# A short matmul of 144 columns ahead of each row of groups of seven products, one of 112 columns in each half of the quads, and the quads' split weights 64 bytes further into their tiles

## The chip, the core and the metric

The kernel runs on one core of one Trainium2 chip. The metric is the time of one execution on the device in microseconds (us). Of the five engines, TensorE (PE, the matrix unit, whose weight loads are listed apart as PEld), VectorE (DVE) and ScalarE (ACT) do the arithmetic; GpSimd (POOL) and SyncE (SP) start transfers (DMAs).

## What is computed

Two layers of a decoder trunk on 512 tokens of width 1024, all in float32. The parts that this document speaks of are the two feed-forward blocks (FFN) of each layer and the mixer's branch gates:

```python
def swiglu(h, w_gate, w_up, w_down):
    return (jax.nn.silu(h @ w_gate) * (h @ w_up)) @ w_down
...
    for l in range(DEPTH):
        h = rms_norm(x, gn[0])
        x = x + 0.5 * rms_norm(swiglu(h, w_ffn1_gate[l], w_ffn1_up[l], w_ffn1_down[l]), gn[1])
        h = rms_norm(x, gn[2])
        proj = h @ w_in[l]
...
        mixed = jax.nn.sigmoid(gate_a) * y_hg + jax.nn.sigmoid(gate_b) * y_at
        x = x + rms_norm(mixed @ w_out[l], gn[3])
        h = rms_norm(x, gn[4])
        x = x + 0.5 * rms_norm(swiglu(h, w_ffn2_gate[l], w_ffn2_up[l], w_ffn2_down[l]), gn[5])
```

D_FF is 2816, that is 22 blocks of 128 columns. Between the two FFNs of a layer stands the mixer: a gated recurrence and a windowed attention, each followed by a projection and a gate.

## The kernel before

**One product is three matmuls.** A float32 matrix is held as a high part (`whi` for weights, rounded to the type fp32r) and a low part (`wlo`, what is left). `mm3` multiplies high by high, high by low and low by high. Each matmul loads its own 128x128 weight block first, so 13531 matmuls come with 13531 weight loads.

**Weights.** `Stream` reads them from memory in tiles `w` of 128x1024 floats by DMAs on SP's queue (four raw buffers, `W32`), and `Stream.split` makes of each an `Item`: a pair `whi`, `wlo` of eight blocks of 128 columns, with six buffers each (`WS`). ACT writes `whi` (line 353). `wlo` comes from a subtraction on DVE (line 362, kinds u, b, c) or from a negated copy on ACT (line 357) and an accumulating DMA that POOL starts (line 360, kinds v, a, d). The tile of an item has 1088 columns, and `at` says at which column the 1024 begin: `pairs` puts its items (kinds a, b, c, d) 16 columns, that is 64 bytes, in (`ASIDE`); `plain` puts its items at column 0.

**Stages.** An FFN begins with a *quad*: four output blocks of 128 columns for all tokens, from four plain items. Where the input was normalised by the stage before (three of the four FFNs, and both mixers), `quad` runs in two halves of 256 tokens, 96 matmuls of 256 columns each, the weights being used twice; late in the first half TensorE turns the second half of the tokens (`turn`). The first FFN does its quad on all 512 tokens. After the quad come a few single blocks (`project`, 512 columns), and then a *row of groups*: `fast` calls `sevenths` once for each further block of D_FF, 15 times in the first FFN and 19 times in the three others. One group makes the gate and the up block with seven products of half size in place of eight: it is 7 x 4 x 3 = 84 matmuls of 256 columns, from four items. The operands that are sums of input quarters come from `pre.sums()` ahead of the row, the sums of weights from DVE inside `split`, and the sums of results from DVE at the end of `sevenths` (lines 1054 to 1061). The order on TensorE is written out by hand; in a row the order on DVE and ACT is held to the program's order too (`hold`, `tight`). After the row comes the down projection (`down`), 512 columns wide, part of which again uses seven products, with sums on DVE (lines 263, 295, 432).

The mixer has a quad, projections, attention and recurrence, and four groups (`branches`), each followed by two products of 512 columns; these groups are single ones, each a row of its own.

In time, the rows of groups of the four FFNs run from 88.6 to 237.0, 729.3 to 915.3, 1063.8 to 1249.0 and 1745.4 to 1933.4 us of the profile. They are called row 1 to row 4 here.

Of the kernel before, what the change touches and what calls it, by code (L numbers as in the profile page):

```python
# [15 lines left out]
P = 128  # L16
# [16 lines left out]
    first=0.0, spread=2300.0, squares=1700.0, lay=34500.0, laid=770.0, normed=7600.0, final=2600.0,  # L33
# [4 lines left out]
TURN = 0  # L38
SEVEN = 16
ASIDE = 16  # L40
ORDER = ("p1", "p3", "p7", "p2", "p6", "p5")
HEADS = (0, 4, 1, 5, 2, 6, 3, 7)

# [2 lines left out]
def trunk(ctx: ExitStack, tc: tile.TileContext, xin, wall, gains, lbT, hgain, sinks, c_dist, c_mask, c_ident, out):  # L46
# [12 lines left out]
    def nm(s):  # L59
        seq[0] += 1  # L60
        return f"{s}_{seq[0]}"

    def big(dt=F32, shape=None):
        return sb.tile(shape or [P, S], dt, tag="s", name=nm("s"), bufs=SLOTS)
# [4 lines left out]
    def acc():  # L69
        return ps.tile([P, S], F32, tag="acc", name=nm("acc"), bufs=5)  # L70

    def aux():
        return ps.tile([P, S], F32, tag="aux", name=nm("aux"), bufs=3)
# [40 lines left out]
    def mm(o, lhsT, rhs, start, stop):  # L114
        nc.tensor.matmul(o, lhsT, rhs, start=start, stop=stop)  # L115
        n = 1
        for d in rhs.shape[1:]:
            n *= d
        if rhs.dtype == F32:
            order.t += max(n / 2.4, 27.0) * (2 if lhsT.shape[1] == 64 and n < 256 else 4)  # L120
        else:
            order.t += max(n / 2.4, 107.0)
# [35 lines left out]
    class Stream:  # L158
# [10 lines left out]
            self.side, self.freed = [], 0  # L169
            self.part = {}  # L170

        def plain(self, n, kind="u"):
            self.items += [Item(kind, self.n + i) for i in range(n)]
            for i in range(n):
                self.src.setdefault(self.n + i, self.wall + i)
            self.n += n
            self.wall += n

        def pairs(self, n, at=ASIDE):

            for _ in range(n):
                self.items += [Item(k, self.n, 4 if k == "d" else 8, at) for k in "abcd"]
                for i in range(2):
                    self.src.setdefault(self.n + i, self.wall + i)
                self.n += 2
                self.wall += 2

        def gates(self):
# [6 lines left out]
            self.plain(1)  # L195

        def rows(self, kt, fast):


# [15 lines left out]
            if fast:  # L215
# [6 lines left out]
                def product(k):  # L222
                    for q in range(n):
                        it = Item(k, u, 4)
                        it.q, it.n = q, n
                        self.items.append(it)

                for k in ORDER:
                    product(k)
# [179 lines left out]
    ws = Stream()  # L409

    def mm3(o, st, mv, start, stop):

        mm(o, st[0], mv[0], start, False)
        mm(o, st[0], mv[1], False, False)
        mm(o, st[1], mv[0], False, stop)

    def wmm(o, b, mv, start, stop, poll=True):

        mm3(o, b[2:], mv, start, stop)
        ws.used(b)  # L420
        if poll:
            order.poll()

    def cut(pair, c):
        return pair[0][:, c], pair[1][:, c]
# [222 lines left out]
    class Late:  # L648
# [42 lines left out]
        def leave(self, n, k):  # L691
# [4 lines left out]
            elif n in (5, 7):  # L696
                (self.x37 if n == 7 else self.x56)[k] = None

    def down(src, kt, l, n, nxt, fast):


# [292 lines left out]
    def quad(pre, halves):  # L994

        o = [acc() for _ in range(4)]
        blocks = {}
        ws.pinned = halves
        for half in (0, 1) if halves else (None,):
            c = WHOLE if half is None else HALF[half]  # L1000
            for k in range(KT):
                order.until(lambda: pre.have[half or 0] > k)
                for j in range(4):
                    if (k, j) not in blocks:
                        blocks[k, j] = ws.next(uses=2 if halves else 1)
                    wmm(o[j][:, c], blocks[k, j], cut(pre.h[k], c), k == 0, k == KT - 1)
            ws.pinned = False
        return o
# [17 lines left out]

    H2 = S // 2

    def sevenths(pre, between=lambda: None):

        def product(o, it, c, n):
            x = pre.operand(n)
            for k in range(4):
                wmm(o, ws.block(it, c + k), x[k], k == 0, k == 3)

        p1, p26, p57, p43 = acc()[:, :H2], acc(), acc(), aux()
        s, v = big()[:, :H2], big(F32, [P, 2, H2])
        w = ws.whole()  # L1040
        product(p1, w, 0, 1)
        ws.hold(nc.scalar.copy(s, p1))
        product(p26[:, :H2], w, 4, 2)
        between()
        w = ws.whole()
        product(p57[:, :H2], w, 0, 5)
        product(p57[:, H2:], w, 4, 7)
        c = ws.whole()
        product(p26[:, H2:], c, 0, 6)
        ws.product()  # L1050
        m = sb.tile([P, 4, H2], F32, tag="m", name=nm("m"), bufs=1)
        pairs = [p.rearrange("p (i t) -> p i t", i=2) for p in (p26, p57, p43)]

        ws.hold(nc.vector.tensor_tensor(m[:, 0:4:2, :], pairs[0], s.unsqueeze(1).to_broadcast([P, 2, H2]), op=ALU.add))

        ws.hold(nc.vector.tensor_tensor(v, pairs[1], m[:, 2:3, :].to_broadcast([P, 2, H2]), op=ALU.add))
        product(p43[:, :H2], c, 4, 4)
        product(p43[:, H2:], ws.whole(), 4, 3)

        ws.hold(nc.vector.tensor_tensor(m[:, 3, :], p57[:, :H2], v[:, 1, :], op=ALU.add))  # L1060
        ws.hold(nc.vector.tensor_tensor(m[:, 1:3, :], pairs[2], v[:, ::-1, :], op=ALU.add))
        return m

    def fast(pre, a, start):
        def early():
            if j == FT - 1:
                for i in range(SEVEN, SEVEN + EARLY):
                    ws.part[i] = split(a[i])

        ws.tight = True  # L1070
        for j in range(start, FT):
            ws.most = AHEAD + (j < FT - 1)
            m = sevenths(pre, early)
            z = big(F32, [P, 2, H2])
            ws.hold(nc.scalar.activation(out=m[:, 0:2, :], in_=m[:, 0:2, :], func=AF.Silu))

            def gate(m=m, z=z):
                ws.hold(nc.vector.scalar_tensor_tensor(z, m[:, 0:2, :], -1.0, m[:, 2:4, :], op0=ALU.mult, op1=ALU.mult))

            ws.gate = gate  # L1080
            if j == FT - 1:
                ws.product()
            a.append(z.rearrange("p i t -> p (i t)"))
        ws.tight = False

    def ffn(l, n, pre, nxt, halves=True):
# [13 lines left out]

        first = isinstance(pre, First)
        o = quad(pre, halves)
        if first:
            o.append(project(pre))
# [152 lines left out]
    def mixer(l, pre, nxt):  # L1257
# [40 lines left out]
        def run(i, heads):  # L1298
# [8 lines left out]
            for n in range(2):  # L1307
                order.spawn(outputs(i + n, box[n]), n * WAIT["apart"])

        o = quad(pre, True)  # L1310
        order.spawn(run(0, [head(o[2 * i], o[2 * i + 1], i) for i in range(2)]))

# [125 lines left out]
        def branches(get):  # L1438

            v = sevenths(pre)  # L1440
            src = get()
            for i in range(2):
                g = big(F32, [P, 2, H2])
                nc.scalar.activation(out=g, in_=v[:, 2 * i : 2 * i + 2, :], func=AF.Tanh, scale=-0.5 if i else 0.5)
                p = acc()
                for k in range(4):
                    wmm(p, ws.next(), src[k], k == 0, k == 3)
                g = g.rearrange("p i t -> p (i t)")
                nc.vector.scalar_tensor_tensor(g, g, 1.0, p, op0=ALU.add, op1=ALU.mult)
                yield g  # L1450
# [23 lines left out]
    for l in range(DEPTH):  # L1474
        for n in (0, 2, 4):
            if n == 2:
                ws.plain(4, "v")
                ws.plain(2 * H + 2 + 8 + LATE * 3 // 2)
                for _ in range(KT - LATE // 2):
                    ws.gates()  # L1480
                ws.rows(KT, False)
            else:
                p = FIRST if l + n == 0 else 3
                ws.plain(4, "v" if l and not n else "u")
                ws.plain(min(2 * p, 8) - 4)
                ws.plain(max(2 * p - 8, 0), "v")
                ws.pairs(FT - p)
                ws.rows(FT, True)
    pre = First()
# [68 lines left out]
    for l in range(DEPTH):  # L1558
        pre = ffn(l, 0, pre, (l, 2), halves=l > 0)
        pre = mixer(l, pre, (l, 4))  # L1560
        pre = ffn(l, 4, pre, (l + 1, 0) if l + 1 < DEPTH else None)
# [81 lines left out]
```

## Time and profile before

| | us |
|---|---|
| median of 3 runs | 2056.75 |
| lowest and highest | 2055.87, 2056.76 |
| the profiled execution | 2057.03 |
| its span in the profile | 2055.3 |
| TensorE busy | 2044.0 |
| weight loads busy | 1831.3 |
| DVE busy | 1624.1 |
| ACT busy | 1250.1 |
| clock granted to TensorE | full in all 40 slices |

The span runs from the first to the last recorded instruction; 1.7 us of the execution lie around it. A matmul's bar in the profile is longer than the distance to the next one, since matmuls overlap in the engine's pipeline, so a busy TensorE says nothing of its pace. The pace is read from the starts: the timeline gives the start of each matmul, and the view by stretches counts the matmuls of a stretch (it counts those that reach into it too, about two more than begin in it).

### The profile page before, as it was taken

To read this page: it belongs to the slowest core of one execution; us is meant where nothing else is said; L and a number is where in the kernel's file an instruction comes from. 1 tells how busy PE (TensorE), PEld (TensorE's weight loads), DVE (VectorE), ACT (ScalarE), POOL (GpSimd) and SP (SyncE) were. 2 spreads that over 40 slices of the span, in tenths; PEclk is the share of its full clock that TensorE was granted. 3 is DMA by queue.
4 is the path that set the end of the run, shared out by engine and by line. 5 is a ranking of instruction groups with operands and counts; after the bars stand their busy time and mean duration, and the time that the engine had idled before them with its cause. 6 is when DMAs were issued, how large, how long until landed. Compare 5 with 4: busy or idle time off the path is not lost. (4 is left out here: it accounts for less than half of the span.)

```text
span 2055.3 us, 36503 instructions
## 1 busy us (share of the span) xinstructions
PE 2044.0 (99%) x13531; PEld 1831.3 (89%) x13531; DVE 1624.1 (79%) x2894; ACT 1250.1 (61%) x2213; POOL 267.6 (13%) x318
## 2 busy tenths in 40 slices
PE   9999999999999999999999999999999999999998
PEld 7899988877888999997899998888778989999987
DVE  5887889767676778888988788977686858788888
ACT  7556687446355556658866566864554545665684
POOL 0111140000000012113201111400000100111140
PEclk9999999999999999999999999999999999999999
DMA  8587798312247367879857778872122563788794
GB/s 256 148 188 191 175 206 239 114 64 70 73 101 207 113 151 189 189 187 208 206 151 189 192 187 207 177 232 85 62 73 62 140 193 99 181 189 195 176 199 123
DMA packets 166802, 328.07 MB, mean 160 GB/s; under 512 B 19072, under 2 KB 85088, under 8 KB 166624
## 3 DMA queue, kind: packets, MB, share of 16 engines
q1 hardware_dynamic: 122416, 228.16, 33.3%
q0 software_dynamic: 44064, 97.54, 28.2%
q8 instruction: 106, 1.74, 0.4%
q14 instruction: 72, 0.59, 0.1%
q10 hardware_dynamic: 144, 0.05, 0.0%
HBM read 213.43 MB, written 14.73 MB: 111 GB/s over the span
## 5 line engine op out<-in xcount | busy, mean ns | idle before, releaser
L115 PE MATMUL acc<-s,whi 128*128 128x256 f32 (+1 forms) x4976 | 1035.9, 306 | 0.4 <-ACT whi L353 0.4
L115 PEld LDWEIGHTS acc<-s,whi 128*128 128x128 f32 x4976 | 799.7, 189 | 47.2 <-issue 3.2
L115 PE MATMUL acc<-s,wlo 128*128 128x256 f32 (+1 forms) x2488 | 760.5, 306 | 1.0 <-DMA wlo<-w 0.8
L115 PEld LDWEIGHTS acc<-s,wlo 128*128 128x128 f32 x2488 | 468.9, 188 | 25.1 <-DMA wlo<-w 1.5
L115 PE MATMUL acc<-whi,s 128*128 128x512 f32 x1360 | 442.0, 393 | 1.4 <-DVE s L432 1.3
L353 ACT CAST whi<-w 128x1024 fp32r<-128x1024 f32 (+1 forms) x310 | 286.4, 928 | 151.0 <-PE acc L115 102.9
L353 ACT CAST whi<-tt 128x1024 fp32r<-128x1024 f32 x160 | 167.9, 1049 | 250.7 <-DVE tt L347 177.8
L360 POOL DMA_DIRECT2D wlo<-w x178 | 154.0, 867 | 1237.3 <-ACT wlo L357 532.0
L115 PEld LDWEIGHTS acc<-whi,s 128*128 128x128 f32 x1360 | 255.2, 188 | 59.6 <-issue 3.2
L362 DVE TENSOR_TENSOR wlo<-tt,whi 128x1024 fp32r<-128x1024 f32 x160 | 196.0, 1225 | 131.6 <-ACT whi L353 124.6
L115 PE MATMUL acc<-wlo,s 128*128 128x512 f32 x680 | 266.3, 392 | 1.2 <-DVE wlo L295 1.2
L115 PE MATMUL aux<-s,whi 128*128 128x256 f32 (+1 forms) x1296 | 233.1, 281 | 0.0
L362 DVE TENSOR_TENSOR wlo<-w,whi 128x1024 fp32r<-128x1024 f32 (+1 forms) x132 | 157.6, 1207 | 75.6 <-ACT whi L353 74.6
L115 PEld LDWEIGHTS aux<-s,whi 128*128 128x128 f32 x1296 | 199.1, 189 | 1.1 <-issue 0.5
L115 PE MATMUL aux<-s,wlo 128*128 128x256 f32 (+1 forms) x648 | 182.2, 281 | 0.0
L115 PEld LDWEIGHTS acc<-wlo,s 128*128 128x128 f32 x680 | 127.7, 188 | 30.0 <-DVE wlo L295 5.2
L357 ACT ACTIVATE wlo<-w 128x1024 fp32r<-128x1024 f32 (+1 forms) x178 | 153.7, 863 | 0.0
L115 PE MATMUL aux<-whi,s 128*128 128x512 f32 x432 | 143.8, 390 | 0.0
L443 POOL DMA_DIRECT2D s<-s x128 | 111.0, 969 | 218.4 <-ACT s L431 98.6
L115 PEld LDWEIGHTS aux<-s,wlo 128*128 128x128 f32 x648 | 121.9, 188 | 0.3
L295 DVE TENSOR_TENSOR wlo<-s,whi 128x512 fp32r<-128x512 f32 x160 | 103.0, 690 | 9.9 <-ACT whi L287 8.1
L431 ACT CAST s<-s 128x512 fp32r<-128x512 f32 (+1 forms) x140 | 70.8, 548 | 44.8 <-DVE s L490 39.3
(184 smaller groups left out, 2468.8 us busy)
## 6 DMA issues: line engine op xcount, KB each, us to landing
w<-wall SPq DMA_DIRECT2D x267, 512.0 KB, 4.2
wlo<-w POOLq DMA_DIRECT2D x98, 512.0 KB, 5.2
w<-wall SPq DMA_DIRECT2D x224, 128.0 KB, 3.6
wlo<-w POOLq DMA_DIRECT2D x80, 256.0 KB, 3.2
s<-wall SPq DMA_DIRECT2D x128, 128.0 KB, 4.1
s<-s POOLq DMA_DIRECT2D x64, 256.0 KB, 4.6
x_d<-s SPq DMA_DIRECT2D x48, 256.0 KB, 4.2
s<-x_d SPq DMA_DIRECT2D x48, 256.0 KB, 5.2
```

The lines of the kernel that those rows point to most:

```text
L115: nc.tensor.matmul(o, lhsT, rhs, start=start, stop=stop)
L295: pin(nc.vector.tensor_tensor(it.lo[:, h[c]], w[c], it.hi[:, h[c]].bitcast(F32), op=ALU.subtract))
L353: i = nc.scalar.copy(it.hi[:, c], w[:, c])
L357: i = nc.scalar.mul(it.lo[:, c], w[:, c], -1.0)
L360: nc.gpsimd.dma_start(it.lo[:, c].bitcast(F32), w[:, c], accum_op=ALU.add)
L362: self.hold(nc.vector.tensor_tensor(it.lo[:, c], w[:, c], it.hi[:, c].bitcast(F32), op=ALU.subtract))
L431: (hold or ws.hold)(nc.scalar.copy(hi, src))
L443: nc.gpsimd.dma_start(lo.bitcast(F32), src, accum_op=ALU.add)
```

## The change

```diff
+LEAD, LEAD_IN = 144, 112
...
-        def plain(self, n, kind="u"):
-            self.items += [Item(kind, self.n + i) for i in range(n)]
+        def plain(self, n, kind="u", at=0):
+            self.items += [Item(kind, self.n + i, at=at) for i in range(n)]
...
                 for j in range(4):
                     if (k, j) not in blocks:
                         blocks[k, j] = ws.next(uses=2 if halves else 1)
+                    if halves and (k, j) == (0, 2):
+                        lead(o[j][:, c], blocks[k, j][2], pre.h[k][0][:, c], LEAD_IN)
                     wmm(o[j][:, c], blocks[k, j], cut(pre.h[k], c), k == 0, k == KT - 1)
...
-    def sevenths(pre, between=lambda: None):
+    def lead(o, st, mv, n):
+        mm(o[:, :n], st, mv[:, :n], True, True)
+
+    def sevenths(pre, between=lambda: None, first=True):
...
         w = ws.whole()
+        if first:
+            lead(p1, w.hi[:, :P], pre.operand(1)[0][0], LEAD)
         product(p1, w, 0, 1)
...
-            m = sevenths(pre, early)
+            m = sevenths(pre, early, j == start)
...
-                ws.plain(4, "v")
+                ws.plain(4, "v", ASIDE)
...
-                ws.plain(4, "v" if l and not n else "u")
+                ws.plain(4, "v" if l and not n else "u", ASIDE if l + n else 0)
```

`lead` is one more matmul, with the same weight block and the first columns of the same input as the matmul behind it, and into the same accumulator, which that matmul then starts afresh; so its result is overwritten. It stands ahead of the first group of each FFN's row (4 times) and ahead of each group of the mixers (8 times) with 144 columns, and ahead of the third block's first product in each half of the five quads that run in halves (10 times) with 112 columns. The four items of these five quads now begin at column 16 of their tiles. The quad of the first FFN stays as it was.

On DVE, ACT, POOL and SP the instructions stand in the same order as before, and on TensorE nothing is moved but for the 22 added matmuls. This is TensorE at the start of row 1, where the 512 columns of the last `project` end and the first group begins (`s` is the input, 880 and 918 are two accumulators), before:

```order
L115 MATMUL acc_880<-s_186,wlo_704 128x512
L115 MATMUL acc_880<-s_199,whi_703 128x512
L115 MATMUL acc_880<-s_200,whi_703 128x512
L115 MATMUL acc_880<-s_199,wlo_704 128x512
L115 MATMUL acc_918<-s_598,whi_766 128x256 x2
L115 MATMUL acc_918<-s_598,wlo_767 128x256
L115 MATMUL acc_918<-s_623,whi_766 128x256 x2
```

and now:

```order
L116 MATMUL acc_880<-s_186,wlo_704 128x512
L116 MATMUL acc_880<-s_199,whi_703 128x512
L116 MATMUL acc_880<-s_200,whi_703 128x512
L116 MATMUL acc_880<-s_199,wlo_704 128x512
L116 MATMUL acc_918<-s_598,whi_766 128x144
L116 MATMUL acc_918<-s_598,whi_766 128x256 x2
L116 MATMUL acc_918<-s_598,wlo_767 128x256
L116 MATMUL acc_918<-s_623,whi_766 128x256 x2
```

One matmul of 144 columns stands between the last wide one and the first of the group. And this is TensorE in the second quad of the program, at the start of its first half (4133 to 4136 are the four accumulators, 4029 and 4030 the input's high and low part), before:

```order
L115 MATMUL acc_4133<-s_4029,whi_3918 128x256
L115 MATMUL acc_4133<-s_4030,whi_3918 128x256
L115 MATMUL acc_4133<-s_4029,wlo_3919 128x256
L115 MATMUL acc_4134<-s_4029,whi_3918 128x256
L115 MATMUL acc_4134<-s_4030,whi_3918 128x256
L115 MATMUL acc_4134<-s_4029,wlo_3919 128x256
L115 MATMUL acc_4135<-s_4029,whi_3918 128x256
L115 MATMUL acc_4135<-s_4030,whi_3918 128x256
```

and now (all numbers of names are one higher):

```order
L116 MATMUL acc_4134<-s_4030,whi_3919 128x256
L116 MATMUL acc_4134<-s_4031,whi_3919 128x256
L116 MATMUL acc_4134<-s_4030,wlo_3920 128x256
L116 MATMUL acc_4135<-s_4030,whi_3919 128x256
L116 MATMUL acc_4135<-s_4031,whi_3919 128x256
L116 MATMUL acc_4135<-s_4030,wlo_3920 128x256
L116 MATMUL acc_4136<-s_4030,whi_3919 128x112
L116 MATMUL acc_4136<-s_4030,whi_3919 128x256
L116 MATMUL acc_4136<-s_4031,whi_3919 128x256
```

Six matmuls run first, then the one of 112 columns, then the quad goes on as it did.

## The prediction

> **What bounds the kernel now.** I read the page first, then the timeline of TensorE for its pace, then the counts by stretch, then DVE and ACT beside it.
>
> ```profile
> span 2055.3 us, 36503 instructions
> PE 2044.0 (99%) x13531; PEld 1831.3 (89%) x13531; DVE 1624.1 (79%) x2894; ACT 1250.1 (61%) x2213; POOL 267.6 (13%) x318
> ```
>
> TensorE hardly ever stands still, so what counts is how far apart its matmuls start. The same matmul of 256 columns has three paces. Below, from the timeline (start, length, engine, line, operation, tiles, shape, count), are the first and last line of a stretch in row 1, one in row 2 and one in a quad:
>
> ```profile
> 205.15 0.40 PE L115 MATMUL aux<-s,whi 128*128 128x256 f32 x2
> ...
> 211.51 0.40 PE L115 MATMUL acc<-s,whi 128*128 128x256 f32 x2
> ...
> 790.29 0.39 PE L115 MATMUL acc<-s,whi 128*128 128x256 f32 x2
> ...
> 796.41 0.39 PE L115 MATMUL aux<-s,whi 128*128 128x256 f32 x2
> ...
> 348.48 0.40 PE L115 MATMUL acc<-s,whi 128*128 128x256 f32 x2
> ...
> 355.68 0.40 PE L115 MATMUL acc<-s,whi 128*128 128x256 f32 x2
> ```
>
> Row 1: 54 matmuls in 6.36 us, 117.8 ns each. Row 2: 54 in 6.12 us, 113.3 ns. Quad: 60 in 7.20 us, 120.0 ns. Nothing waits inside these stretches and the clock is full; only the quad's weights begin at column 0 of their tiles. So 117.8 and 113.3 are two paces of the same work, and the counts by stretch show when they change:
>
> ```profile
> 88.60:237.00 148.40, 148.40 (x1262) 1.00 0.79 191
> 602.50:612.20 9.70, 9.70 (x86) 1.00 0.96 240
> 760.00:788.00 28.00, 28.00 (x248) 1.00 0.81 193
> 790.00:845.00 55.00, 55.00 (x488) 1.00 0.81 191
> 847.00:915.00 68.00, 68.00 (x580) 1.00 0.79 193
> 1125.00:1199.00 74.00, 74.00 (x655) 1.00 0.81 192
> 1221.00:1249.00 28.00, 28.00 (x240) 1.00 0.75 188
> 1745.40:1933.40 188.00, 188.00 (x1597) 1.00 0.78 189
> ```
>
> With two taken off each count, rows 1 and 4 run at 117.8 from end to end; row 2 runs at 113.8 and 113.2 between 760 and 845 and at 117.6 afterwards; row 3 at 113.3 from 1125 and at 117.6 from 1221. Each change stands at a place where a weight load was late; one of them (weight loads, the idle time before in brackets):
>
> ```profile
> 788.70 0.19 PEld L115 LDWEIGHTS acc<-s,wlo 128*128 128x128 f32 x1 [0.81 <-DMA wlo<-w]
> 788.80 0.30 PEld L115 LDWEIGHTS acc<-s,whi 128*128 128x128 f32 x2
> ```
>
> So the pace is set by a phase that an interruption deals anew and undisturbed work keeps. A lead of another length is such an interruption, without a wait. That is what the change can act on.
>
> **But a faster TensorE runs into DVE.** In a row DVE and ACT prepare the weights in turns, and each group shows the same loop:
>
> ```profile
> 741.44 0.68 DVE L1054 TENSOR_TENSOR m<-acc,s 128x512 f32<-128x512 f32 x1
> ...
> 746.29 1.23 DVE L362 TENSOR_TENSOR wlo<-tt,whi 128x1024 fp32r<-128x1024 f32 x1 [0.59 <-ACT whi L353]
> ...
> 750.04 1.22 DVE L362 TENSOR_TENSOR wlo<-tt,whi 128x1024 fp32r<-128x1024 f32 x1 [1.19 <-ACT whi L353]
> 751.18 0.68 DVE L1054 TENSOR_TENSOR m<-acc,s 128x512 f32<-128x512 f32 x1
> ...
> 799.71 0.68 DVE L1054 TENSOR_TENSOR m<-acc,s 128x512 f32<-128x512 f32 x1
> ...
> 809.42 0.68 DVE L1054 TENSOR_TENSOR m<-acc,s 128x512 f32<-128x512 f32 x1
> ```
>
> Line 1054 comes once a group: 9.74 us apart where TensorE ran at 117.8, 9.71 where it ran at 113.3. A group of 84 takes TensorE 9.89 us at the one pace and 9.52 at the other. The loop, which waits for ACT and not for TensorE, lies between. It also keeps its place from row to row:
>
> ```profile
> 729.33 0.40 PE L115 MATMUL acc<-s,whi 128*128 128x256 f32 x2
> ...
> 909.26 0.68 DVE L1061 TENSOR_TENSOR m<-aux,s 128x512 f32<-128x512 f32 x1
> ...
> 1745.44 0.40 PE L115 MATMUL acc<-s,whi 128*128 128x256 f32 x2
> ...
> 1925.35 0.68 DVE L1061 TENSOR_TENSOR m<-aux,s 128x512 f32<-128x512 f32 x1
> ```
>
> The same late sum of DVE stands 179.93 us behind the start of row 2 and 179.91 behind that of row 4, though row 2 spent half its time at 113.3 and ended 186.0 us after its start, row 4 188.0. What row 2 had won it gave back in the down projection. The first 53 us of the four down projections, by count (TensorE, weight loads, DVE, ACT, POOL):
>
> ```profile
> 237.00:290.00 53.00, 53.00 (x235) 43.88 (x235) 46.58 (x94) 38.88 (x82) 16.42 (x19) 1.00 0.86 204
> 915.30:968.30 53.00, 52.07 (x228) 42.16 (x227) 46.84 (x94) 37.31 (x80) 15.30 (x18) 1.00 0.85 206
> 1249.00:1302.00 53.00, 51.56 (x223) 41.16 (x222) 47.96 (x94) 37.15 (x78) 14.11 (x17) 1.00 0.86 206
> 1933.40:1986.40 53.00, 53.00 (x236) 43.90 (x235) 45.80 (x92) 37.43 (x80) 15.76 (x19) 1.00 0.85 205
> ```
>
> Behind rows 1 and 4 TensorE gets 235 and 236 matmuls done, behind the two that ran partly at 113.3 228 and 223. At 227 ns each (53 us over 234) that is 1.6 and 2.8 us of waiting, for DVE:
>
> ```profile
> 942.43 0.30 PEld L115 LDWEIGHTS acc<-whi,s 128*128 128x128 f32 x2 [1.04 <-DVE s L432]
> ...
> 946.96 0.19 PEld L115 LDWEIGHTS aux<-wlo,s 128*128 128x128 f32 x1 [0.62 <-DVE wlo L295]
> ```
>
> So in an FFN the bound is already DVE's and ACT's chain, with TensorE close on its heels.
>
> **The change, part by part.** *The leads* add 22 matmuls. A lead waits for the accumulator, weights and input for which the matmul behind it waits anyway, so no wait is added, and no DMA and nothing on POOL's or SP's queue moves. Each loads weights, so it costs at least the 0.10 us between two crowded weight loads (788.70 to 788.80 above) and at most a product at the worst pace, 0.12. I take 0.11: 0.9 us in the mixers' rows, 1.1 in the quads, 0.4 in the FFN rows.
>
> *The quads.* 10 halves x 96 = 960 matmuls, now at 120.0. With the weights 64 bytes in they are in the rows' situation, so 113.3 or 117.8: a gain of 6.4 or 2.1 us for all, 1.28 or 0.43 a quad. I take 113.3, since a lead stands in each half. Less 0.22 for two leads that is 1.06 a quad. In the two mixers I let all of it count, 2.1 us: TensorE has hardly a gap there. In the three FFNs DVE must follow, and only part of its chain hangs on the quad. It waits for the turned tokens in the middle of the quad, then is held by ACT:
>
> ```profile
> 703.79 0.88 DVE L629 SCALAR_TENSOR_TENSOR s<-acc,g_sb,s 128x256 fp32r<-128x256 f32 x2 [0.63 <-PE aux L125]
> ...
> 712.40 1.29 DVE L432 TENSOR_TENSOR s<-s,s 128x512 fp32r<-128x512 f32 x2 [1.39 <-ACT s L431]
> ```
>
> The first wait has 0.63 us to give; the turn comes after 72 of the faster matmuls, 0.5 us earlier. I take 0.6 a quad, 1.8 for three. Quads together 3.9 us, bounded by 0 (DVE does not move, the mixers wait too) and 5.3 (all of it counts).
>
> *The mixers' groups.* Eight of 84, of which one ran at 113.3 already (602.50 to 612.20 above, 84 in 9.7 us with a wait in it). Seven x 84 x 4.44 ns = 2.6 us, less 0.9 for leads: 1.7. Bounds: -0.9 (the lead changes nothing) and 1.7 (nothing waits).
>
> *The FFN rows.* TensorE alone would win 5.6 us in row 1 (15 groups x 0.37), 7.1 in row 4, 5.1 in row 2 and 4.3 in row 3, whose stretches at 113.3 count already. DVE's loop stops this at 9.71 us a group, and the down projection takes most of the rest, as in rows 2 and 3. Row 2 is the measure: it came out of its row 2.0 us earlier than row 4 and lost 1.6 behind it. I give 0.4 to row 4, the same and 1.0 more to row 1, where the loop starts with more lead and TensorE never waits, 0.6 to row 3 for the bigger wait, nothing to row 2: 2.4 us. The leads are hidden here behind the same DVE work; were DVE's cover gone they would cost 0.4. Bounds: 0 and 22.
>
> Sum: 3.9 + 1.7 + 2.4 = 8.0 us off the profiled execution's 2057.03: 2049.0. That execution lies 0.3 us above the median of 2056.75, less than the sum is good for.
>
> **The rivals.** *A. TensorE is the bound after all.* For it: 99% busy. Then the rows keep their 22, the mixers 1.7, the quads 5.3, less 0.4: 2028. Against it: what became of row 2's gain. Chance 0.07.
>
> *B. The leads do not set the pace.* A late load does not always bring 113.3 (at 847 and 1221 it brought 117.6), and nothing in the trace says what 144 or 112 columns do. Then only the offset acts: 2.1 us less 2.4 for leads, no change, 2057; or one of the two leads works and the other not: 2053. Chance 0.17, most of it within 2052 to 2057.
>
> *C. Weights and inputs do not disturb each other at all, the paces have another cause, and the 64 bytes do nothing.* Then 22 x 0.11 = 2.4 us is all that remains: 2059.4. Against it: 120.0 in the quads beside 117.8 in the rows, with the same shapes. Chance 0.06. [...]
>
> *D. Slower: a lead locks a row into the quads' 120.0.* Then a group takes 10.08 us, more than DVE's loop of 9.71, and TensorE is the bound again. From 9.89 that is 0.19 x 15 = 2.8 us in row 1, 3.6 in row 4, 4.0 in row 2, which had kept 0.4, 3.6 in row 3, which had kept nothing, 1.9 in the mixers' groups and 2.4 for leads, the quads staying as they are: 18.3, so 2075. It decides from the first group on. Against it: no group at offset 16 shows 120 anywhere. Chance 0.06.
>
> **The numbers.** My forecast has 0.64: 2049.0, in its own range from 2042 (the quads' 5.3, row gains of 8) to 2054 (half the quads' gain, nothing from the rows). The range for 8 in 10 leaves out A, C and D, 0.19: 2041 to 2056.5. 0.2%, or 4.1 us, is about what a measurement of this kernel can tell from no change. Faster by more: 0.60 of my 0.64, A's 0.07, 0.07 of B: 0.74. Slower by more: D's 0.06 and 0.03 from C, were a lead to cost three times as much: 0.09. Within: 0.17.
>
> **What would show it.** The rows, counted by stretch, should run at 113.3 ns from their first group, with late loads of `wlo<-w` in rows 1 and 4 too, which have none now. Line 1054 on DVE should still come every 9.71 us. The first 53 us of all four down projections should hold 223 to 229 matmuls, with waits for lines 432 and 295. The quads should show 113.3 behind their leads. I am wrong if line 1054 comes closer together than 9.7 us or the down projections show no wait (then A), if rows start at 117.8 (B), or if quads stay at 120.0 (C).

## The result, and the profile after

| | before | after |
|---|---|---|
| median of 20 runs each, us | 2056.44 | 2052.96 |
| lowest and highest | 2055.45, 2057.69 | 2051.33, 2053.96 |
| ratio, 95% interval | | 0.9983 [0.9976, 0.9989] |
| the profiled execution | 2057.03 | 2052.22 |
| its span | 2055.3 | 2050.4 |

The change makes the kernel 3.5 us faster. That is 0.17%: the interval of the ratio excludes no change, but the median lies inside the band of 0.2% that the prediction called "within" and gave 0.17, against 0.74 for a gain beyond it. The forecast was 2049.0, 8.0 us below the profiled execution of before; by the medians less than half of that came. In the two profiled executions the difference is 4.8 us, because the one of before happened to lie 0.6 us above its median and the one of after 0.7 below; the parts below are counted in these two.

The first lines of the page of after (busy time, share of the span, instructions):

```profile
span 2050.4 us, 36557 instructions
PE 2035.9 (99%) x13553; PEld 1820.7 (89%) x13553; DVE 1623.6 (79%) x2894; ACT 1250.1 (61%) x2213; POOL 267.6 (13%) x318
```

TensorE has 22 matmuls more and is busy for 8.1 us less, while DVE's busy time is the same. Where it went is read by stage. These are the four rows of after and the first 53 us behind each (stretch, its length, TensorE, weight loads, DVE, ACT, POOL, then granted clock, DMA share, GB/s):

```profile
88.60:233.40 144.80, 144.80 (x1262) 144.80 (x1261) 116.08 (x163) 89.09 (x122) 24.95 (x29) 1.00 0.79 191
233.40:286.40 53.00, 51.70 (x225) 41.49 (x224) 47.55 (x94) 37.30 (x79) 14.72 (x17) 1.00 0.85 205
728.10:915.20 187.10, 186.94 (x1599) 186.42 (x1598) 150.43 (x210) 115.12 (x158) 31.85 (x37) 1.00 0.78 188
915.20:968.20 53.00, 52.69 (x232) 42.89 (x231) 46.85 (x95) 38.36 (x81) 16.13 (x19) 1.00 0.88 213
1062.30:1247.00 184.70, 182.66 (x1599) 181.52 (x1598) 147.71 (x208) 113.16 (x156) 31.84 (x37) 1.00 0.77 187
1247.00:1300.00 53.00, 50.90 (x221) 40.59 (x220) 48.40 (x95) 37.43 (x78) 13.86 (x16) 1.00 0.86 211
1741.60:1927.90 186.30, 185.73 (x1598) 185.23 (x1597) 149.62 (x210) 115.03 (x158) 31.84 (x37) 1.00 0.78 189
1927.90:1980.90 53.00, 52.25 (x229) 42.30 (x229) 46.74 (x94) 37.35 (x79) 15.35 (x18) 1.00 0.85 208
```

Row 1 takes 144.8 us where it took 148.4. But behind it TensorE gets 225 matmuls done in 53 us, where it got 235 before. Row 4 takes 186.3 (188.0 before), and 229 matmuls follow (236 before). Rows 2 and 3 are about as long as they were (1.1 us longer and 0.5 shorter).

Stage by stage, from the starts of the first matmuls of the stages in both timelines (a row counts with its down projection, up to the next stage):

| us against before | forecast | measured |
|---|---|---|
| row 1 and behind it | -1.4 | -0.35 (row -3.6, behind it +3.2) |
| row 2 and behind it | 0 | +0.06 (row +1.1, behind it -1.0) |
| row 3 and behind it | -0.6 | -0.38 |
| row 4 and behind it | -0.4 | -0.92 (row -1.6, behind it +0.7) |
| five quads | -3.9 | -2.19 (-0.44 each) |
| first mixer, second mixer | -1.7 in all | -0.09 and -1.00 |
| sum | -8.0 | -4.8 (with +0.04 ahead of row 1) |

**The paces of a row.** The counts of after, by pieces of the four rows (two matmuls are to be taken off each count, as before):

```profile
88.60:183.00 94.40, 94.40 (x834) 94.40 (x833) 75.83 (x107) 57.67 (x78) 17.21 (x20) 1.00 0.79 189
190.00:233.40 43.40, 43.40 (x370) 43.40 (x370) 34.52 (x49) 26.78 (x38) 6.02 (x7) 1.00 0.80 194
...
788.00:915.00 127.00, 127.00 (x1081) 127.00 (x1080) 103.31 (x144) 78.54 (x108) 21.53 (x25) 1.00 0.78 190
...
1123.00:1245.00 122.00, 121.89 (x1072) 121.50 (x1071) 97.98 (x139) 73.93 (x101) 21.53 (x25) 1.00 0.80 193
...
1743.00:1760.00 17.00, 17.00 (x152) 17.00 (x151) 12.66 (x19) 9.93 (x15) 2.98 (x4) 1.00 0.73 155
1762.00:1799.00 37.00, 37.00 (x317) 37.00 (x316) 30.37 (x43) 23.20 (x32) 6.88 (x8) 1.00 0.79 185
1801.00:1857.00 56.00, 56.00 (x494) 56.00 (x495) 45.84 (x65) 34.94 (x48) 10.32 (x12) 1.00 0.78 188
1859.00:1927.00 68.00, 68.00 (x578) 68.00 (x579) 54.82 (x77) 42.76 (x60) 11.18 (x13) 1.00 0.77 190
```

Row 1 starts at 113.5 ns a matmul (832 in 94.4 us) and ends at 117.9. Row 4 starts at 113.3, goes at 117.5 from 1762, at 113.8 from 1801 and at 118.1 from 1859. Both were at 117.8 from end to end before. Row 2 starts at 113.3 too, but from 788 to its end it goes at 117.7 (1079 in 127 us), where before it had kept 113.3 until 846; that is why it is longer now. Row 3 starts at 113.3 and never leaves it: its 122 us from 1123 on hold 1070 matmuls and a few short waits. Four of the ten weight loads that the profile lists as late in the rows and the groups of the mixers (idle time before them in brackets), one in the first mixer's second group, one in row 3 and two in row 4:

```profile
602.42 0.19 PEld L116 LDWEIGHTS acc<-s,wlo 128*128 128x128 f32 x1 [0.67 <-DMA wlo<-w]
...
1110.94 0.19 PEld L116 LDWEIGHTS acc<-s,wlo 128*128 128x128 f32 x1 [0.51 <-DMA wlo<-w]
...
1761.15 0.19 PEld L116 LDWEIGHTS acc<-s,wlo 128*128 128x128 f32 x1 [0.25 <-DMA wlo<-w]
...
1858.82 0.19 PEld L116 LDWEIGHTS acc<-s,wlo 128*128 128x128 f32 x1 [0.71 <-DMA wlo<-w]
```

The pace falls at 1761 and at 1859, behind these loads. In row 1 no load is listed as late; its pace falls at 184.1, where the start of one matmul behind a `wlo` load slips by 45 ns. But not every late load changed the pace: in row 3 five are late, by 0.17 to 1.77 us, and behind each TensorE goes on at 113.3; in row 2 one at 757.92 brings 113.3 back.

Row 3 also says what sets the time. TensorE could do its 1596 matmuls in 180.9 us at 113.3 and needs 184.7, which is 9.72 a group, DVE's loop (19 x 9.71 is 184.5). And though nothing throws it back to 117.8, only 0.38 us of gain is left in its stage.

**DVE's loop** is where it was. The sum at the head of each group, line 1063 now (1054 before), in rows 1 and 4 of after:

```profile
118.22 0.68 DVE L1063 TENSOR_TENSOR m<-acc,s 128x512 f32<-128x512 f32 x1
127.93 0.68 DVE L1063 TENSOR_TENSOR m<-acc,s 128x512 f32<-128x512 f32 x1
...
1821.85 0.68 DVE L1063 TENSOR_TENSOR m<-acc,s 128x512 f32<-128x512 f32 x1
1831.56 0.68 DVE L1063 TENSOR_TENSOR m<-acc,s 128x512 f32<-128x512 f32 x1
```

9.71 us apart, in rows in which TensorE could do a group in 9.52. What TensorE gains it waits for behind the row, for DVE (lines 296 and 433 were 295 and 432):

```profile
261.24 0.30 PEld L116 LDWEIGHTS acc<-whi,s 128*128 128x128 f32 x2 [1.12 <-DVE s L433]
265.77 0.19 PEld L116 LDWEIGHTS aux<-wlo,s 128*128 128x128 f32 x1 [0.62 <-DVE wlo L296]
...
1275.83 0.30 PEld L116 LDWEIGHTS acc<-whi,s 128*128 128x128 f32 x2 [1.09 <-DVE s L433]
```

**A quad.** TensorE in the second quad of the program, after the change, around the first half's lead and then at the first and last line of an undisturbed stretch in each half:

```profile
348.05 0.28 PE L116 MATMUL acc<-s,wlo 128*128 128x256 f32 x1
348.17 0.51 PE L116 MATMUL acc<-s,whi 128*128 128x112 f32 x3
348.52 0.28 PE L116 MATMUL acc<-s,wlo 128*128 128x256 f32 x1
...
349.33 0.39 PE L116 MATMUL acc<-s,whi 128*128 128x256 f32 x2
...
355.45 0.39 PE L116 MATMUL acc<-s,whi 128*128 128x256 f32 x2
...
361.54 0.40 PE L116 MATMUL acc<-s,whi 128*128 128x256 f32 x2
...
369.67 0.40 PE L116 MATMUL acc<-s,whi 128*128 128x256 f32 x2
```

The line with x3 is the lead and two products: 0.35 us, where two alone take 0.24 at 117.8, so a lead costs 0.11 us, as assumed. First half: 54 matmuls in 6.12 us, 113.3 ns. Second half: 69 in 8.13 us, 117.8 ns, although it has a lead too.

### The profile page after: what moved, and what is told of

It is laid out like the page before. It is cut to its first block, busy times and chain, and to the rows that moved or that the text cites. A ratio compares the mean times of both kernels' runs of the same rounds, so it can differ in the third digit from the quotient of the medians.

```text
span 2050.4 us, 36557 instructions
## 1 busy us (share of the span) xinstructions
PE 2035.9 (99%) x13553; PEld 1820.7 (89%) x13553; DVE 1623.6 (79%) x2894; ACT 1250.1 (61%) x2213; POOL 267.6 (13%) x318
```

## The experiments

The theory (W, where an expectation uses a letter): a lead sets the pace of what follows; in the FFN rows DVE's and ACT's loop of 9.71 us takes the gain back. The rival (R): TensorE is the bound, and the gain is lost because late loads throw the rows back to 117.8.

### The parts alone

Three kernels take parts of the change away. Rows only: no leads in the quads and their items at column 0.

```diff
-                    if halves and (k, j) == (0, 2):
-                        lead(o[j][:, c], blocks[k, j][2], pre.h[k][0][:, c], LEAD_IN)
...
-                ws.plain(4, "v", ASIDE)
+                ws.plain(4, "v")
...
-                ws.plain(4, "v" if l and not n else "u", ASIDE if l + n else 0)
+                ws.plain(4, "v" if l and not n else "u")
```

> The changed kernel with its twelve leads of 144 columns alone; the quads as before. Theory W (the leads set the pace of 113.3 ns until a late load deals it anew, and in the four FFN rows the loop of DVE and ACT, 9.71 us a group, gives nearly all of it back): mixers' groups at 113.3, rows start at 113.3, quads stay at 120.0, 2054.0 us (2053 to 2055), 2.5 below the kernel before. Rival R (TensorE is the bound, and what is missing is only the groups that fall back to 117.8): 2048 or less, since the rows alone would then be worth over 8 us.

Quads only: no leads ahead of the groups.

```diff
-        if first:
-            lead(p1, w.hi[:, :P], pre.operand(1)[0][0], LEAD)
```

> The changed kernel without the leads ahead of the groups: quads at column 16 with their leads of 112. W: first halves at 113.3, second halves at 117.8 as in the changed kernel, rows and mixers' groups back at 117.8: 2054.3 us (2053.5 to 2055), 2.2 below before; e1 and e2 together add up to the whole change (about 3.5 to 4.7). R: the same here, it speaks of the rows.

Offset only: neither kind of lead (both edits to `lead` above), the quads' items at column 16.

> No lead anywhere, the quads' items at column 16. If the lead sets the quads' pace (W): both halves at 117.8, 960 matmuls x 2.2 ns = 2.1 us on TensorE, about 1 to 1.5 us in the end: 2055.0 us. If the offset alone does it: first halves at 113.3 and the time of e2 or 0.5 us less, since ten leads are saved: 2053.8 us.

| | median, us (before 2056.59) | ratio, 95% interval | a quad, us (24.77 before) | second mixer's group, us (9.89 before) |
|---|---|---|---|---|
| rows only | 2054.21 | 0.9987 [0.9978, 0.9996] | 24.77 | 9.64 |
| quads only | 2054.76 | 0.9988 [0.9980, 0.9997] | 24.33 | 9.89 |
| offset only | 2055.38 | 0.9992 [0.9983, 1.0001] | 24.37 | 9.89 |

All three came within 0.5 us of what was expected. The third interval still holds no change, so what the offset alone brings is read from the quads and not from the median. With the offset alone both halves of the quads run at 117.8, with items at column 0 at 120.0. So the 64 bytes move 120.0 to 117.8, and the lead moves 117.8 to 113.3. The two leads of a quad bring 0.04 us beyond the offset: only some 61 of the 192 products run at 113.3, between the first lead and the place where TensorE turns the second tokens; the 24 behind that are at 117.8 again, and the second half's lead leaves the pace there. Against 61 x 4.5 ns, 0.27 us, stand two leads of 0.11.

Row 1 of rows only, and the 53 us behind it:

```profile
88.80:232.40 143.60, 143.52 (x1262) 143.15 (x1261) 114.86 (x162) 87.90 (x121) 25.00 (x29) 1.00 0.79 189
232.40:285.40 53.00, 50.71 (x220) 40.47 (x219) 48.17 (x96) 36.88 (x76) 13.90 (x16) 1.00 0.84 209
```

Here the pace of 113.3 lasts to the end of the row (143.6 us, 148.4 before), through a late load of 0.28 us at 213.39. What follows the row is 4.5 us longer than before, and 0.28 us of gain is left. This and row 3 above speak for W: with the loop of 9.71 us as it is, the gain goes even where no late load throws TensorE back.

### A lead ahead of every group

```diff
-            m = sevenths(pre, early, j == start)
+            m = sevenths(pre, early)
```

> The changed kernel with a lead of 144 columns ahead of every group of the FFN rows (76 in place of 4). W: every group then runs at 113.3 from its start until its late load, but the loop still takes 9.71 us a group, and a group with its lead 9.63: the waits for wlo grow and the time stays within 1 us of the changed kernel, 2052 to 2054 us. R: the 30 or so groups that now run at 117.8 gain 0.37 us each, 11 us, less 72 leads of 0.11: 2049 us or less.

Measured 2054.85, ratio 0.9989 [0.9981, 0.9998]: 0.85 us above the range of W and far above that of R, for a reason that neither theory had. The leads in row 1 of this kernel, from its timeline (each line is the lead and two products):

```profile
98.41 0.51 PE L116 MATMUL acc<-s,whi 128*128 128x144 f32 x3
...
108.41 0.51 PE L116 MATMUL acc<-s,whi 128*128 128x144 f32 x3
...
118.06 0.51 PE L116 MATMUL acc<-s,whi 128*128 128x144 f32 x3
...
128.07 0.51 PE L116 MATMUL acc<-s,whi 128*128 128x144 f32 x3
```

10.00, 9.65 and 10.01 us apart: the groups take turns, 84 matmuls at 117.8 and 84 at 113.3, in all four rows. Inside these rows a lead of 144 columns did not set a pace; it turned one into the other, both ways. The mean group takes 9.83 us, more than the loop of 9.71, so only one load is listed as late in the four rows, and the run says nothing for W or R. It only corrects the first half of W: here a lead ahead of a group changed the pace that it met.

### The bound: DVE's loop shortened

In a row DVE waits twice a group for ACT (0.59 and 1.19 us in the prediction's rows). The second wait comes because DVE sums the weights of item c only after it has subtracted for item b, so ACT gets c late. Two additions, moved ahead:

```diff
             if it.kind == "b":
...
                 pin(nc.vector.tensor_tensor(self.t13[:, h[1]], v[:, h[0]], v[:, h[1]], op=ALU.add))
+                t = self.t2 = sb.tile([P, D], F32, tag="tt", name=nm("tt"), bufs=2)
+                pin(nc.vector.tensor_tensor(t[:, h[0]], self.t13[:, h[0]], v[:, h[1]], op=ALU.add))
+                pin(nc.vector.tensor_tensor(t[:, h[1]], t[:, h[0]], w[:, h[1]], op=ALU.add))
                 w = self.t13
                 self.product()
             elif it.kind == "c":
-                t = sb.tile([P, D], F32, tag="tt", name=nm("tt"), bufs=2)
-                pin(nc.vector.tensor_tensor(t[:, h[0]], self.t13[:, h[0]], v[:, h[1]], op=ALU.add))
-                pin(nc.vector.tensor_tensor(t[:, h[1]], t[:, h[0]], w[:, h[1]], op=ALU.add))
-                w = t
+                w = self.t2
```

(The items b and c of a pair are made from the same two raw tiles, so `w` and `v` are the same in both places.) First in the kernel before, without leads and offset:

> The kernel before, with one thing moved on DVE: the two additions that make the weight sum of an item c (lines 346 and 347) stand ahead of the low part of item b, so that DVE works where it waited 0.59 and 1.19 us for ACT. Same arithmetic, no lead, no offset. W: DVE's loop falls from 9.71 to 8.0 to 8.5 us a group; no weight load of a row is late, so all four rows keep the 117.8 ns with which they begin (188 us in rows 2 to 4), and the waits in the down projections vanish: 2056 us (2054 to 2057.5), no change. R (late loads come from the DMAs, not from the loop): late loads stay, 2056.5 us.

Measured 2055.20, ratio 0.9992 [0.9983, 1.0001]: alone the move is worth next to nothing. DVE in row 2 of this kernel:

```profile
756.50 0.69 DVE L1054 TENSOR_TENSOR m<-acc,s 128x512 f32<-128x512 f32 x1 [0.97 <-PE acc L115]
...
759.32 0.69 DVE L1061 TENSOR_TENSOR m<-aux,s 128x512 f32<-128x512 f32 x1 [0.95 <-PE aux L115]
...
766.39 0.69 DVE L1054 TENSOR_TENSOR m<-acc,s 128x512 f32<-128x512 f32 x1 [0.97 <-PE acc L115]
```

The loop comes every 9.89 us now, which is TensorE's group at 117.8, and DVE waits for TensorE twice a group, 0.97 and 0.95 us. Without these waits the loop would take 8.0 us, as expected. No load of a row is late, and all four rows stay at 117.8 (rows 2 to 4 188.0 us each).

Then in the changed kernel:

> The changed kernel with the same two additions moved. W: with the loop out of the way the leads' 113.3 ns lasts through all four rows, 145 us in row 1 and 181 in rows 2 to 4, 27 us less on TensorE than in e5, of which the down projections may take some back: 2030 us (2026 to 2042). R: the rows fall back at late loads as now, and the time is the changed kernel's, 2052 to 2053 us.

Measured 2025.88, ratio 0.9853 [0.9838, 0.9868], 30.6 us below before in the medians. Row 2 and the 53 us behind it, by stretch, then DVE in that row:

```profile
722.80:903.70 180.90, 180.90 (x1598) 180.90 (x1597) 151.35 (x214) 116.80 (x155) 30.09 (x35) 1.00 0.78 189
903.70:956.70 53.00, 53.00 (x236) 43.89 (x235) 46.59 (x94) 38.39 (x82) 16.49 (x19) 1.00 0.85 204
```

```profile
758.40 0.69 DVE L1063 TENSOR_TENSOR m<-acc,s 128x512 f32<-128x512 f32 x1 [0.70 <-PE acc L116]
...
764.86 2.35 DVE L363 TENSOR_TENSOR wlo<-tt,whi 128x1024 fp32r<-128x1024 f32 x2
767.92 0.69 DVE L1063 TENSOR_TENSOR m<-acc,s 128x512 f32<-128x512 f32 x1 [0.70 <-PE acc L116]
```

1596 matmuls in 180.9 us, 113.3 ns, from the first group to the last, in all four rows. The two subtractions of line 363 stand side by side, the loop comes every 9.52 us, and DVE waits for TensorE even at that pace. 236 matmuls follow in 53 us, as behind an undisturbed row, and the time is 0.1 us below the range of W. So W holds in its main point: with the loop out of the way the leads and the offset are worth 29.3 us (2055.20 to 2025.88), with it 3.5. R falls: with the shorter loop no load is late in any row of this run, and with the old one the gain was lost in two rows that no late load had thrown back. How much of the loss in rows 2 and 4 of the changed kernel the fall back to 117.8 adds to the loop's is not shown.

### Other lengths, one run

Leads of other lengths: 64, 80, 176 and 240 columns ahead of the four FFN rows; 16, 48, 96, 112, 128, 160, 208 and 256 ahead of the mixers' groups; 64, 96, 128, 144 and 160 in the halves of the five quads.

```diff
-LEAD, LEAD_IN = 144, 112
+LEADS, LEADS_IN = [64, 16, 48, 96, 112, 80, 176, 128, 160, 208, 256, 240], [64, 64, 96, 96, 128, 128, 144, 144, 160, 160]
...
-            lead(p1, w.hi[:, :P], pre.operand(1)[0][0], LEAD)
+            lead(p1, w.hi[:, :P], pre.operand(1)[0][0], LEAD.pop(0))
```

> The changed kernel with leads of other lengths, to read the pace behind each: rows 1 to 4 of the FFNs 64, 80, 176, 240 columns, the eight groups of the mixers 16, 48, 96, 112 and 128, 160, 208, 256, both halves of the five quads 64, 96, 128, 144, 160. If a lead flips the phase whatever its length (one matmul more): 113.3 behind all of them, and the quads' second halves stay at 117.8. If the length decides: lengths of an odd number of 16 columns (16, 48, 80, 112, 144, 176, 208) give 113.3 and even ones (64, 96, 128, 160, 240, 256) 117.8. The time says little; about 2053 us.

One run, 2053.18. Pace behind each lead, from the starts in its timeline:

| place | 113.3 ns | 117.8 ns |
|---|---|---|
| ahead of a row or a group | 16 to 240 columns, all eleven | 256 |
| first half of a quad | 64, 96, 128, 144, 160 (and 112) | none |
| second half of a quad | 64, 96 | 128, 144, 160 (and 112) |

Neither expectation came. It is not enough that there is one more matmul (256 does nothing), and the length decides otherwise only in the second halves, where 64 and 96 do what 112 and more don't. The pace ahead does not explain that: in both halves of a quad the matmuls ahead of the lead run at 117.8. Each length was tried once in its place, in one run, and why they differ is not settled.

### 64 columns in the second halves

The kernel with the sums moved, and this:

```diff
-                        lead(o[j][:, c], blocks[k, j][2], pre.h[k][0][:, c], LEAD_IN)
+                        lead(o[j][:, c], blocks[k, j][2], pre.h[k][0][:, c], 64 if half else LEAD_IN)
```

> The changed kernel with the two additions on DVE moved ahead (as in the run with both, 2025.88), and in the second half of the five quads a lead of 64 columns in place of 112; the first halves keep 112. Which pace a lead leaves hangs on its length and on the pace ahead of it: then the second halves go from 118.5 to 113.5 ns behind their leads (90 matmuls of each), 5 x 90 x 4.8 ns = 2.2 us for TensorE. Where TensorE is the bound in the quads as it is in the rows now, all of it counts: 2023.7, range 2023.2 to 2024.8. If DVE sets the end of the quads in the FFNs (my prediction's view, three of the five), only the two mixers' 0.9 counts: 2025.0. If the second halves stay at 117.8, nothing: 2025.9.

Measured 2023.76 (2023.15 to 2027.25), ratio 0.9840 [0.9827, 0.9854]: 2.1 us below the kernel with the sums moved alone, as expected where all of it counts. The two intervals overlap, so the gain rests on the quads' own times below. The profiled execution was the slowest of the five and shows both what the edit gains and how a run loses it. A second half without the edit (90 matmuls) and with it (91), by stretch, each from its own kernel:

```profile
356.50:367.10 10.60, 10.60 (x92) 10.60 (x92) 3.67 (x3) 4.78 (x5) 0.00 (x0) 1.00 0.37 133
```

```profile
356.40:366.70 10.30, 10.30 (x93) 10.30 (x92) 3.67 (x3) 4.67 (x5) 0.00 (x0) 1.00 0.41 141
```

Each of the five quads takes 23.95 us now (24.33 without the edit), and row 4 starts 1.5 us earlier. Then, in row 4 (one late load; the stretches before and after it):

```profile
1825.27 0.19 PEld L116 LDWEIGHTS acc<-s,wlo 128*128 128x128 f32 x1 [0.28 <-DMA wlo<-w]
```

```profile
1720.00:1824.00 104.00, 104.00 (x920) 104.00 (x918) 88.71 (x127) 67.19 (x89) 18.07 (x21) 1.00 0.76 180
1827.00:1904.30 77.30, 77.30 (x659) 77.30 (x658) 61.05 (x85) 47.43 (x64) 11.17 (x13) 1.00 0.82 199
```

113.3 ns before it, 117.7 behind it, to the end of the row. A wait of 0.28 us cost 3.3 us of row (184.3 against 180.9). DVE waits for TensorE 0.70 us a group there too, so its loop is not what lags; where the late load comes from is not shown.

### Every weight at column 0

```diff
-ASIDE = 16
+ASIDE = 0
```

in the changed kernel, leads as they are: this is the prediction's rival D, priced by itself.

> The changed kernel with every item at column 0 of its tile, pairs and quads alike; leads of 144 and 112 as they are. If the weights' column decides between 120.0 and the two other paces and a lead cannot leave 120.0 (rival D's price, but for the weights' place and not for the lead): the groups of the four rows take 84 x 120.0 = 10.08 us, rows 151.2, 191.5, 191.5, 191.5 us against 144.7, 187.1, 184.7, 186.3 now, 22.9 us more, less some 5 that the down projections have less to wait for; the mixers' groups 8 x 84 x 6.0 ns = 4.0; the quads 960 x 4.5 ns = 4.3; the wide matmuls perhaps 6 ns of 227 more, some 30 us over 5000 of them: 2075 to 2110, at 2080 if the wide ones keep their pace. If the lead sets 113.3 whatever the column (120.0 was then the quads' own phase): 2053, as the changed kernel.

Measured 2071.81, ratio 1.0073 [1.0055, 1.0092]. Row 1, what follows it, row 2 and a mixer's group, by stretch:

```profile
88.40:239.60 151.20, 151.20 (x1262) 151.20 (x1261) 119.82 (x167) 91.45 (x124) 24.94 (x29) 1.00 0.78 187
733.80:925.40 191.60, 191.60 (x1599) 191.60 (x1598) 152.68 (x213) 116.39 (x158) 31.84 (x37) 1.00 0.78 186
...
239.60:344.50 104.90, 104.90 (x464) 86.65 (x463) 96.08 (x180) 81.55 (x170) 29.87 (x35) 1.00 0.81 198
590.00:600.10 10.10, 10.10 (x86) 10.10 (x85) 7.57 (x10) 6.26 (x8) 1.72 (x2) 1.00 0.61 140
```

In every stretch read the products of 256 columns run at 120.0 ns (1260 in 151.2 us, 1596 in 191.6), each lead notwithstanding, and the granted clock is 1.00. The products of 512 columns take as long as before (104.9 us behind row 1); their split weights stood at column 0 in every kernel here, so the run does not try what the place does to them. The time is 8 us below the 2080 that was expected for that case. The rows came out 23.1 us longer than in the changed kernel, as expected (22.9), but the stretches behind them took back 10.0 us and not 5, and quads and mixers lost 6.9 and not 8.3. At column 0 one pace was read, 120.0 ns; 64 bytes further two, 113.3 and 117.8, and a lead changed one into the other.

The gains by stage against the profile of before, one profile each, from the same marks as in the first table ("all" is the difference of the spans, with up to 0.34 us ahead of row 1):

| us | rows 1 to 4, each with what follows | five quads | two mixers | all |
|---|---|---|---|---|
| after | -0.35, +0.06, -0.38, -0.92 | -2.19 | -0.09, -1.00 | -4.8 |
| rows only | -0.28, +0.07, -0.55, -1.01 | 0.00 | -0.34, -0.99 | -2.8 |
| quads only | +0.21, +0.28, -0.26, -0.74 | -2.18 | +0.40, 0.00 | -2.2 |
| offset only | -0.12, +0.12, +0.09, +0.46 | -1.99 | +0.30, -0.01 | -1.5 |
| sums moved, before | -0.07, -0.27, -1.16, -0.66 | 0.00 | +0.22, 0.00 | -2.0 |
| sums moved, after | -4.73, -6.86, -8.20, -8.09 | -2.19 | -0.78, -1.02 | -32.1 |
| column 0 | +2.82, +4.02, +2.49, +2.21 | +1.07 | +1.39, +1.17 | +14.9 |

## Why the prediction was right in kind and too high in size

**The bound.** Right, and shown. The prediction held that in the FFNs DVE's and ACT's loop of 9.71 us is the bound, with TensorE close behind. The loop kept its 9.71 us, and what row 1 won was waited for behind it, as were the gains of rows that no late load had thrown back (row 3 of after, row 1 of rows only). Rival A (2028, TensorE the bound) was wrong for this kernel and right for the one in which the loop is shorter: 2025.88.

**The rows, 2.4 us forecast, 1.6 measured.** The right order of size, but spread wrongly: row 1 was given 1.4 for the head start of its loop and kept 0.35, row 4 was given 0.4 and shows 0.92. Such shares are good to half a microsecond at best: quads only and offset only have no lead ahead of a row, and their row 4 shows -0.74 and +0.46, their four rows together -0.51 and +0.55. So it is not shown that row 4's 0.92 is the lead's, and part of the agreement in the sum may be luck. The working also has one reading wrong: the late load at 788.70, shown there as one at which the pace changes, has 113.3 on both sides.

**The quads, 3.9 us forecast, 2.2 measured.** This is the term that was mis-sized most. "I take 113.3, since a lead stands in each half": some 305 of the 960 matmuls run at 113.3, because behind the turn late in the first half the pace is 117.8 again and the second half's lead of 112 columns does not change it back. That the lower of the two values, 0.43 a quad, is so near the measured 0.44 is chance: the offset alone brought 0.40, and the first half's 0.27 at 113.3 paid for the two leads. The gain of a quad stayed below the cap of 0.6 that the prediction set for the FFNs, so the cap was not tried. With 64 columns and the shorter loop, where TensorE is the bound, the quads gained 0.81 each.

**The mixers' groups, 1.7 us forecast, 1.1 measured.** In the second mixer 1.0, as large as assumed for four groups (4 x 0.25). In the first mixer three groups should have gained 0.25 each; they did, but the second group, which ran at 113.3 before too, now had a wait of 0.67 us for a `wlo` load, took 0.7 us longer and gave most of it back.

**What the profile should show.** Rows at 113.3 from the first group: yes. Late loads of `wlo<-w` in rows 1 and 4: in row 4 two, in row 1 only the slip of 45 ns, and it was enough to end the pace. Line 1054 every 9.71 us: yes. 223 to 229 matmuls in the first 53 us of each down projection, with waits for 432 and 295: 225, 232, 221 and 229, two of them just outside, with these waits. 113.3 behind the quads' leads: in the first halves, up to the turn.

**The rivals.** B (the leads do not set the pace) was half right, in the second halves and in what a lead is: ahead of every group of a row it changed the pace that it met (9.65 and 10.00 us in turns). Its second form, one of the two leads works and the other not, was put at 2053, and 2052.96 was measured; no sum was given for it, so the closeness is partly luck. C fell in what it forecast, that the 64 bytes do nothing: they are worth 2.0 us in the quads alone, and 19 us where the items of the quads and of all groups go back to column 0. Whether weights and inputs disturb each other, its first half, stays open: the runs show that the place of the weights counts (120.0 ns a matmul at column 0, 113.3 or 117.8 at column 16), and not what it meets. D (a row locked at 120.0) did not come, but its price was tried: 2071.81, where 2075 had been worked out, and by rows 2.82, 4.02, 2.49 and 2.21 us of loss where 2.8, 4.0, 3.6 and 3.6 stood.

## What to carry to other kernels

Here two engines were within 2% of each other (9.71 us a group for DVE's loop, 9.89 or 9.52 for TensorE), and speeding up one of them showed almost nothing, and so did speeding up the other: -3.5 us and -1.3 us apart (the second is not told from nothing), -30.6 us together. Read the period of the slower loop from one of its lines (9.71 us), compare it with the faster engine's best (9.52) and shorten the loop first; the move of two additions that took waits of 0.59 and 1.19 us out of it did that without any instruction more. Read TensorE's pace from its starts, per stretch, and look for the stretches in which the same shape runs faster.

## What the hardware showed that was not expected

- The same fp32r matmul of 256 columns, each with a weight load, has three paces at a granted clock of 1.00: 113.3, 117.8 and 120.0 ns. With weights at the first column of their tile it was 120.0 in every stretch read; 64 bytes further it was one of the other two.
- Between these two a lead of 144 columns ahead of every group of a row switched, both ways (groups of 9.65 and 10.00 us in turns). The pace also changed behind a late load of 0.28 us (113.3 to 117.7) and behind a slip of 45 ns (113.5 to 117.9), but behind five late loads of 0.17 to 1.77 us in row 3 it stayed at 113.3. With the sums moved and no load of a row late, rows 2 to 4 kept one pace to their end: 1596 matmuls in 188.0 us in the kernel before, in 180.9 in the changed one. That a phase sets the pace is the prediction's reading of such stretches; no run shows it.
- From 16 to 240 columns all lengths worked ahead of a group. In the second halves of the quads 64 and 96 worked, 112 and more did not, though the pace ahead was the same as in the first halves, where all that were tried worked. This stays open, as does what other offsets than 64 bytes would do; neither was tried further.
